# Encoder layer on one core: B's weights requested two ahead, and steps of the tail, the memory norm and cross attention moved

## The chip, the core and the metric

The kernel runs on one NeuronCore of a Trainium2 chip. The core has five engines that work side by side, each through its own queue, in order: TensorE (PE) multiplies matrices, and its weight loads (PEld) run ahead of the products; VectorE (DVE) and ScalarE (ACT) do elementwise work; GpSimd (POOL) here mostly issues DMAs; SyncE (SP) issues DMAs alone. An instruction that waits holds everything behind it on its engine. The metric is the device time of one execution in microseconds (us), less is better.

## The reference

One layer of an encoder on 256 frames (SEQ) of width 2048 (D), everything in float32:

```
h = LN(alpha*h + 0.5*SwiGLU_1(h))
h = LN(alpha*h + W_out[ sig(g_A)*(A(h) W_oA) + sig(g_B)*(B(h) W_oB) ])
h = LN(alpha*h + CrossAttn(h, LN(mem)))
h = LN(alpha*h + 0.5*SwiGLU_2(h))
```

A is chunked attention with a relative bias (16 heads of 64). B is latent attention (16 heads; queries and keys have 128 "nope" and 64 rotary columns, values 128). Queries, latents and gates of A and B come from one combined projection. Cross attention has 4 heads of 512 over 256 memory tokens, which get a layer norm of their own. The feed-forward layers are 5504 wide. Almost all the time goes into products of 256 rows with weight matrices that are each read once.

## The kernel before

**Weights.** Each weight matrix is cut into tiles of 128 x 2048 float32 (1 MB). `run` walks a list of items in the order in which they are to use weights. For weight number i, `fetch(i)` asks for the tile by a DMA on SP (L191) into one of three raw buffers (`wraw`). `load(i)` splits it: ACT casts it to a rounded high part in two pieces of 128 x 1024 (`hi`, L261), then DVE subtracts to get the low part (`lo`, L264). There are two pairs of buffers for hi and lo. PE multiplies hi with both halves of the activations and lo with the high half, which makes 24 products of 512 columns for a full weight ("a unit" below). Some weights go by named blocks instead of the two pairs; their tags name the blocks (X0 and X1, for example).

**Shared sums.** Some groups of weights use a Strassen-like product (`mm_sums`, L362), for which DVE first adds quarters of the weight (`weight_sums`, L245 and L247). The sums stand in a third raw buffer, or in a named block where the third entry of the tags names one; then they are cast to X2 (ACT) and X3 (DVE), like a weight.

**Totals and turns.** A product's two halves lie in PSUM. ACT copies one (L282) and DVE adds the other (L283); only then is the PSUM bank free. Four banks (`ps_mm`) and four more (`ps_at`) are used in rotation. Activations that must be turned are cut into 16-bit planes by ACT (`planes`, L839), sent by DMA transposes on SP (`send`, L843) and joined by ACT (`join`, L847).

**B's heads.** Items for the weights of queries' and keys' nope part (w_nope) and values (w_v) alternate with scores (L1026), softmax, turns and products with the values (L1080). While `early` is set, `load(i)` also asks for weight i + 1. Without it a weight is asked for when its load comes up.

**Cross attention.** In this order: keys 0 to 7, two query groups, value group 0, keys 8 to 15, value group 1, output projection. Side steps (sends, joins, `ready` which splits a head's queries, `scores`, `out`, and `gb`, which applies the residual's gain and bias to h) are put between the main steps by tables such as `{4: [join(0), scores(1)]}`: the number says ahead of which main step. The functions of the memory's norm are placed by a table too; `spread` multiplies ones with the diagonals of mean and scale (L1364), `quarter` applies them.

**What sets the order.** The program gives an order and priorities; a scheduler of the language then lays down the final order of each engine by its own costs. `issue_after` puts one instruction behind another one on the same engine.

Of the kernel before, what the change touches and what calls it, by code (L numbers as in the profile page):

```python
# [21 lines left out]
KT = D // P  # L22
# [15 lines left out]
AT_XQ = (4, 6), (2, 4, 6)  # L38
AT_XV = (2, 4, 6), (4, 6)
SUM_HOME = ("X2", "X3"),  # L40
# [59 lines left out]
class Kernel:  # L100
    def __init__(self, ctx, tc, t, out):
        self.tc, self.nc, self.t, self.out = tc, tc.nc, t, out

        def pool(name, bufs=1, **kw):
            return ctx.enter_context(tc.tile_pool(name=name, bufs=bufs, **kw))

        self.const = pool("const")
        self.wraw = pool("wraw", 3)
        self.whi = pool("whi", UNITS)
        self.wlo = pool("wlo", UNITS)  # L110
        self.blocks = pool("blocks")
        self.res = pool("res")
        self.work = pool("work", 4)
        self.small = pool("small", 4)
        self.ps_mm = pool("ps_mm", 4, space=PSUM)
        self.ps_at = pool("ps_at", 4, space=PSUM)
        self.items = []
        self.uid = 0
        self.chain = self.sent = None
        self.cut = self.early = False  # L120


# [54 lines left out]
    def run(self):  # L177
        queue = [w if isinstance(w, (tuple, Sums)) else (w, None) for _, ws, _, _ in self.items for w in ws]
        ready, nxt, live = [], 0, 0

        def slots(w):
            return 0 if isinstance(w, tuple) and w[1] else 1

        raws, sums = {}, {}

        def fetch(i):
            if i not in raws:
                ap = queue[i].ap if isinstance(queue[i], Sums) else queue[i][0]
                raws[i] = self.raw_tile()
                with self.tc.issue_after(self.sent.ins) if self.sent is not None else nullcontext():  # L190
                    self.last_load = self.nc.sync.dma_start(raws[i][:, :ap.shape[1]], ap)  # L191
            return raws[i]

        def form_sums(i):
            if i < len(queue) and isinstance(queue[i], Sums) and i not in sums:
                raw, home = fetch(i), queue[i].stage
                sums[i] = self.weight_sums(raw, queue[i].m, self.block(home, (P, 2048)) if home else self.raw_tile())

        def load(i):
            w = queue[i]  # L200
            raw = fetch(i)
            form_sums(i)
            if isinstance(w, Sums):
                n = 4 * w.m
                got = self.halves(raw[:, w.m:n], *self.unit()), self.halves(
                    sums[i][:, :n], *(self.block(g, (P, 2048), F32R) for g in w.tags))
            else:
                ap, tags = w
                hi, lo = (self.block(g, (P, 2048), F32R) for g in tags[:2]) if tags else self.unit()
                with self.tc.issue_after(self.ln_act.ins) if tags and "turned" in tags else nullcontext():  # L210
                    got = self.halves(raw[:, :ap.shape[1]], hi, lo)
            form_sums(i + 1)
            if self.early and i + 1 < len(queue):
                fetch(i + 1)
            return got

        def early(w):
            return not isinstance(w, Sums) and w[1] is not None and "early" in w[1]

        def ahead(need, held):  # L220
            if nxt < need:
                return True
            n = sum(not early(w) for w in queue[need:nxt])
            return (nxt < need + 5 and (early(queue[nxt]) or n < 2)
                    and held + live + slots(queue[nxt]) <= UNITS)

        done, highs = 0, []
        for fn, ws, held, prio in self.items:
            need = done + len(ws)
            while nxt < len(queue) and ahead(need, held):  # L230
                live += slots(queue[nxt])
                ready.append(load(nxt))
                highs.append(self.last_hi)
                nxt += 1
            got = [ready.pop(0) for _ in ws]
            live -= sum(slots(queue[done + i]) for i in range(len(ws)))
            done = need
            self.next_hi = highs[min(done, nxt - 1)] if highs else None
            self.now_hi = highs[done - 1] if done else None
            with self.prio(prio):  # L240
                fn(*got)
# [563 lines left out]

    def skewed(self, part, steps, tags=None):

        tags = tags or (None, None, ("X0", "X1"), ("X2", "X3"))
        held = [sum(g is None for g in tags[:j]) for j in range(5)]
        for j in range(4):  # L810
            part(0, j, tags=tags[j], held=held[j], keep=True)
        main = self.collect(lambda: [part(1, j, held=held[4] - held[j], again=True) for j in range(4)])
        self.weave(main, dict(zip((0, 3, 4), steps)))
# [516 lines left out]
    def mem_norm(self):  # L1330
# [46 lines left out]
                self.split(v, e["mT"].blk(0, 4 * q, 4), e["mT"].blk(1, 4 * q, 4))  # L1377
            return fn

        return {0: [load], 3: [stat], 6: [spread], 7: [quarter(0)], 9: [quarter(1)], 11: [quarter(2)], 13: [quarter(3)]}  # L1380

    def cross(self, xT, st, steps, steps_out):
        nc, t, e = self.nc, self.t, self.mem
# [15 lines left out]
        def query(g):  # L1399
# [16 lines left out]

            def join(tt):
                return lambda: [self.join(qs["add"][tt, a], turned[g][:, a, tt, :], 512) for a in range(2)]
            self.pair_group(g, t["w_xq"][g], 512, KT, xT, AT_XQ[g], fq, ps, qs)
            self.add(done, prio=SOON)  # L1420
            return {2: [send(0)], 3: [send(1)], 4: [join(0)], 5: [join(1)]}

        def ready(h):
            def fn():
# [7 lines left out]
        def val(g):  # L1432
            ps, qs = {}, {}

            def done():
                for a in range(2):
                    h = 2 * g + a
                    v[h] = self.block(VALUES[h], (P, 2, 2, X_DIM), F32R)
                    for tt in range(2):
                        p = qs["add"][tt, a]  # L1440
                        nc.vector.tensor_tensor(p, p, ps[tt, a], ALU.add)
                        self.split(p, v[h][:, 0, tt, :], v[h][:, 1, tt, :])
            self.pair_group(0, t["w_xv"][g], 512, KT, m, AT_XV[g], fv, ps, qs, None,
                            (("T0", "T1"),) if g else SUM_HOME)
            self.add(done, prio=SOON)

        def scores(h):
# [63 lines left out]
        def keys(a, b):  # L1511
            for j in range(a, b):
# [3 lines left out]
        side = group(query, {1: [form_q(4)], 3: [form_q(6)], 6: [form_q(2)]}, 0)  # L1516
        side = group(query, both(side, {4: [form_v(2)]}), 1)
        group(val, both(side, {2: [form_v(4)], 4: [form_v(6)]}), 0)
        group(keys, {0: [ready(0)], 1: [scores(0), gb(0)], 2: [ready(1), send(0)], 4: [join(0), scores(1)],
                     5: [out(0), ready(2)], 6: [send(1), gb(1)], 7: [gb(2)], 8: [join(1), ready(3), gb(3)]}, 8, KT)  # L1520
        group(val, {1: [out(1), scores(2)], 2: [scores(3)], 3: [send(2)], 4: [send(3)], 5: [join(2)], 6: [join(3)]}, 1)

        def all_items():
            self.out_pair(1, t["w_xo"][0], 0, KT, x, SUMS_XO, fx, True, st, (("T0", "T1"), "T3"))
# [170 lines left out]
```

## Time and profile before

| | us |
|---|---|
| three runs | 2445.43, 2444.67, 2443.38 (median 2444.67) |
| profiled execution | 2444.7 |
| its span | 2442.9 |
| PE busy | 2423.4 (99%) |
| DVE busy | 2121.5 (87%) |
| ACT busy | 1535.3 (63%) |

The span runs from the first instruction to the last. A busy PE means that some product is in flight. PE's idle time of some 20 us is the sum of the stretches in which it waited, the start and the end among them. The table of waits gives for each engine, line and releaser the idle time just before the instruction. DMA engines were busy some 60% of the time with the loads of SP's queue. The granted clock of the run was 0.997 of full.

### The profile page before, as it was taken

The page shows a single profiled execution, that of the slowest core. Times are in us where ns is not written, and L with a number is a line of the kernel's source. Part 1 is how long each engine was busy: PE and PEld are TensorE (multiplying, and loading weights), DVE is VectorE, ACT ScalarE, POOL GpSimd, SP SyncE. Part 2 cuts the span into 40 slices and gives each one's busy share as a digit, 9 for nine tenths or more (in the row PEclk, how much of TensorE's full clock was granted, in tenths as well). Part 3 has the DMA queues.
Part 4 walks back from the last instruction along what each step waited for, and adds up shares of the span by engine and source line. Part 5 has one row for each costly group of instructions (what it writes and reads, how often), then busy time and mean ns, then how long its engine had stood idle before and what let it go on. Part 6 is the DMA issues. An engine that isn't in the chain of part 4 may idle for free.

```text
span 2442.9 us, 29725 instructions
## 1 busy us (share of the span) xinstructions
PE 2423.4 (99%) x11314; PEld 2027.0 (83%) x11314; DVE 2121.5 (87%) x2428; ACT 1535.3 (63%) x2002; POOL 38.7 (2%) x83
## 2 busy tenths in 40 slices
PE   9999999999999999999999999999999999999997
PEld 8888888888888888888888888888888888888886
DVE  8999989899778997788789789889879999888996
ACT  6676755666555557878565567665666675557662
POOL 0000000000000001000000000000000000000000
PEclk9999999999999999999999999999999999999999
DMA  7766656667646657766676556655556766666664
GB/s 267 252 216 216 206 203 210 223 188 233 229 168 207 218 196 241 237 184 170 207 256 224 190 190 198 218 193 185 188 198 216 227 223 207 222 212 204 205 220 165
DMA packets 165854, 513.57 MB, mean 210 GB/s; under 512 B 101168, under 2 KB 101936, under 8 KB 110544
## 3 DMA queue, kind: packets, MB, share of 16 engines
q1 hardware_dynamic: 160256, 493.20, 60.6%
q0 software_dynamic: 4592, 17.30, 2.2%
q8 instruction: 88, 1.44, 0.2%
q10 hardware_dynamic: 864, 1.18, 0.1%
q14 instruction: 54, 0.44, 0.1%
HBM read 485.30 MB, written 2.10 MB: 200 GB/s over the span
## 4 chain that ended last, share of the span: by engine, by line
PE 92%; DVE 3%; ACT 2%; DMA 1%; issue 1%; SPq 0%; DVEq 0%; ACTq 0%; POOL 0%; POOLq 0%
PE at L308 26%; PE mm L308 25%; PE at L362 11%; PE mm L362 11%; PE mm L295 9%; PE mm L274 4%; PE mm L276 2%; ACT hi L261 1%; DVE lo L264 1%; PE at L1026 1%; DMA raw<-w_xk 0%; PE at L416 0%; ACT w L825 0%; PE at L1453 0%; PE at L1080 0%
## 5 line engine op out<-in xcount | busy, mean ns | idle before, releaser
L261 ACT CAST hi<-raw 128x1024 fp32r<-128x1024 f32 (+1 forms) x852 | 804.7, 982 | 466.6 <-PE at L308 157.3
L264 DVE TENSOR_TENSOR lo<-raw,hi 128x2048 fp32r<-128x2048 f32 (+1 forms) x427 | 903.2, 2116 | 148.9 <-ACT hi L261 144.2
L308 PE MATMUL mm<-hi,T 128*128 128x512 f32 (+1 forms) x1328 | 310.8, 384 | 0.0
L308 PEld LDWEIGHTS mm<-hi,T 128*128 128x128 f32 x1328 | 247.6, 188 | 46.5 <-ACT hi L252 0.3
L308 PE MATMUL at<-hi,T 128*128 128x512 f32 x1152 | 275.5, 389 | 0.0
L261 ACT CAST X<-H 128x1024 fp32r<-128x1024 f32 (+1 forms) x166 | 170.7, 1034 | 163.5 <-DVE H L245 129.9
L308 PEld LDWEIGHTS at<-hi,T 128*128 128x128 f32 x1152 | 216.2, 188 | 45.1
L264 DVE TENSOR_TENSOR X<-H,X 128x2048 fp32r<-128x2048 f32 (+1 forms) x83 | 186.9, 2252 | 68.5 <-ACT X L261 68.5
L308 PE MATMUL mm<-lo,T 128*128 128x512 f32 (+1 forms) x664 | 160.4, 382 | 0.0
L308 PEld LDWEIGHTS mm<-lo,T 128*128 128x128 f32 x664 | 123.7, 188 | 22.8
L308 PE MATMUL at<-lo,T 128*128 128x512 f32 x576 | 142.4, 389 | 0.0
L308 PE MATMUL at<-hi,H 128*128 128x512 f32 x560 | 133.7, 389 | 0.0
L308 PEld LDWEIGHTS at<-lo,T 128*128 128x128 f32 x576 | 108.1, 188 | 22.4
L308 PEld LDWEIGHTS at<-hi,H 128*128 128x128 f32 x560 | 105.0, 188 | 21.6
L308 PE MATMUL mm<-hi,H 128*128 128x512 f32 x480 | 114.8, 390 | 1.0 <-DVE w L283 1.0
L247 DVE TENSOR_TENSOR H<-H,raw 128x512 f32<-128x512 f32 (+1 forms) x166 | 112.6, 679 | 2.2
L308 PEld LDWEIGHTS mm<-hi,H 128*128 128x128 f32 x480 | 89.7, 188 | 19.8 <-DVE w L283 1.4
L245 DVE TENSOR_TENSOR H<-raw 128x1024 f32<-128x1024 f32 (+1 forms) x83 | 99.6, 1200 | 1.3 <-DMA raw<-w_gate 0.8
L261 ACT CAST X<-raw 128x1024 fp32r<-128x1024 f32 (+1 forms) x60 | 61.7, 1036 | 56.0 <-DVE raw L247 40.7
L362 PE MATMUL mm<-X,X 128*128 128x512 f32 x342 | 91.1, 392 | 0.0
L362 PE MATMUL at<-X,X 128*128 128x512 f32 (+1 forms) x315 | 82.4, 386 | 0.4 <-ACT X L261 0.4
L264 DVE TENSOR_TENSOR X<-raw,X 128x2048 fp32r<-128x2048 f32 (+1 forms) x30 | 67.5, 2254 | 15.0 <-ACT X L261 13.9
(353 smaller groups left out, 4115.0 us busy)
## 6 DMA issues: line engine op xcount, KB each, us to landing
raw<-ffn_w_in SPq DMA_DIRECT2D x150, 1024.0 KB, 4.9
raw<-ffn_w_out SPq DMA_DIRECT2D x66, 1024.0 KB, 4.9
raw<-w_gate SPq DMA_DIRECT2D x32, 1024.0 KB, 4.8
raw<-ffn_w_out_r SPq DMA_DIRECT2D x16, 1024.0 KB, 5.0
raw<-w_qk SPq DMA_DIRECT2D x16, 1024.0 KB, 5.8
raw<-w_o_b SPq DMA_DIRECT2D x16, 1024.0 KB, 4.9
raw<-w_out SPq DMA_DIRECT2D x16, 1024.0 KB, 4.8
raw<-w_xk SPq DMA_DIRECT2D x16, 1024.0 KB, 5.0
```

The source lines that it names most:

```text
L245: self.nc.vector.tensor_tensor(two[0], two[1], raw[:, :m].unsqueeze(1).to_broadcast([P, 2, m]), ALU.add)
L247: self.nc.vector.tensor_tensor(t[:, a * m:a * m + m], t[:, b * m:b * m + m], raw[:, a * m:a * m + m], ALU.add)
L261: self.last_hi = self.nc.scalar.copy(hi[:, c:d], src[:, c:d])
L264: self.last_lo = self.nc.vector.tensor_tensor(lo[:, :n], src, hi[:, :n].bitcast(F32), ALU.subtract)
L274: self.nc.tensor.matmul(ps, hi[j], x.both(kt), start=(j == 0), stop=False)
L276: self.last_mm = self.nc.tensor.matmul(ps[:, :S], lo[j], x.at(0, kt), start=False, stop=(j == n - 1))
L295: self.last_mm = self.nc.tensor.matmul(ps, x.at(xi, kt)[:, tt * P:(tt + 1) * P], w[wi][:, j * 512 + c:j * 512 + c + m], start=(start and j ...
L308: self.last_mm = self.nc.tensor.matmul(ps[tt, g][:, :n], x.at(xi, kt)[:, tt * P:(tt + 1) * P], w[wi][:, c:c + n], start=first and j + wi + ...
L362: self.last_mm = self.nc.tensor.matmul(bank[:, :m], a[xi], v[wi][:, c * m:(c + 1) * m], start=own and first and wi + xi == 0, stop=own and ...
L1026: nc.tensor.matmul(ps[:, c0:c0 + nk], q[:, tt * P:(tt + 1) * P], k[:, :nk], start=(j == 0), stop=(j == len(parts) - 1))
```

## The change

It has six parts, and no matmul is added or taken away.

1. In B's heads `load(i)` asks for weights i + 1 and i + 2 instead of i + 1 alone.
2. A third tag "next" puts a block's casts behind the last cast of the weight before it (`last_hi`). It is given to the two last weights of the shifted tail of ffn2.
3. In the memory's norm `spread` and the four quarters come one step later.
4. In cross, the sums of query group 0 stand in block H4 and those of value group 0 in block T2, where both stood in a raw buffer.
5. Sends and joins of a query group go to steps 1, 3, 4, 6 (were 2, 3, 4, 5).
6. The side steps of keys 8 to 15 and value group 1 are dealt out anew: scores(0) and gb(0) one step later, gb(1) two earlier, gb(2) one earlier, ready(3) and gb(3) among the values.

The diff, with nothing left out but context:

```diff
@@ run, load(i)
             else:
                 ap, tags = w
                 hi, lo = (self.block(g, (P, 2048), F32R) for g in tags[:2]) if tags else self.unit()
-                with self.tc.issue_after(self.ln_act.ins) if tags and "turned" in tags else nullcontext():
+                first = {"turned": self.ln_act, "next": self.last_hi}.get(tags[2]) if tags and len(tags) > 2 else None
+                with self.tc.issue_after(first.ins) if first else nullcontext():
                     got = self.halves(raw[:, :ap.shape[1]], hi, lo)
             form_sums(i + 1)
-            if self.early and i + 1 < len(queue):
-                fetch(i + 1)
+            for k in range(i + 1, min(i + 3, len(queue)) if self.early else 0):
+                fetch(k)
             return got
@@ skewed
-        tags = tags or (None, None, ("X0", "X1"), ("X2", "X3"))
+        tags = tags or (None, None, ("X0", "X1", "next"), ("X2", "X3", "next"))
@@ the memory's norm
-        return {0: [load], 3: [stat], 6: [spread], 7: [quarter(0)], 9: [quarter(1)], 11: [quarter(2)], 13: [quarter(3)]}
+        return {0: [load], 3: [stat], 7: [spread], 8: [quarter(0)], 10: [quarter(1)], 12: [quarter(2)], 14: [quarter(3)]}
@@ cross, query
-            self.pair_group(g, t["w_xq"][g], 512, KT, xT, AT_XQ[g], fq, ps, qs)
+            self.pair_group(g, t["w_xq"][g], 512, KT, xT, AT_XQ[g], fq, ps, qs, None,
+                            SUM_HOME if g else SUM_HOME + ("H4",))
             self.add(done, prio=SOON)
-            return {2: [send(0)], 3: [send(1)], 4: [join(0)], 5: [join(1)]}
+            return {1: [send(0)], 3: [send(1)], 4: [join(0)], 6: [join(1)]}
@@ cross, val
-                            (("T0", "T1"),) if g else SUM_HOME)
+                            (("T0", "T1"),) if g else SUM_HOME + ("T2",))
@@ cross, the order
-        group(keys, {0: [ready(0)], 1: [scores(0), gb(0)], 2: [ready(1), send(0)], 4: [join(0), scores(1)],
-                     5: [out(0), ready(2)], 6: [send(1), gb(1)], 7: [gb(2)], 8: [join(1), ready(3), gb(3)]}, 8, KT)
-        group(val, {1: [out(1), scores(2)], 2: [scores(3)], 3: [send(2)], 4: [send(3)], 5: [join(2)], 6: [join(3)]}, 1)
+        group(keys, {0: [ready(0)], 2: [scores(0), gb(0)], 3: [send(0), ready(1)], 4: [gb(1)], 5: [join(0), scores(1)],
+                     6: [out(0), ready(2), send(1), gb(2)], 8: [join(1)]}, 8, KT)
+        group(val, {1: [out(1), ready(3), scores(2)], 3: [send(2), scores(3), gb(3)], 5: [join(2), send(3)],
+                    7: [join(3)]}, 1)
```

In the new code lines from 208 to 1418 stand one further down (L843 becomes L844), those of cross attention two and the last ones three. The rows below name tiles by the program's names with their numbers.

SP's queue in the last heads of B, before. The load raw_8883 is the w_nope weight that is issued at 1114.78 us.

```order
L843 DMA_TRANSPOSE w_1331_8617<-H_1303_8465 128x6x128
L843 DMA_TRANSPOSE w_1344_8675<-H_1303_8465 128x6x128
L191 DMA raw_8769<-w_nope 128x2048
L843 DMA_TRANSPOSE w_1353_8725<-H_1303_8465 128x6x128
L843 DMA_TRANSPOSE w_1367_8789<-H_1303_8465 128x6x128
L191 DMA raw_8883<-w_nope 128x2048
L843 DMA_TRANSPOSE w_1376_8839<-H_1303_8465 128x6x128
L191 DMA raw_8945<-w_v 128x2048
L843 DMA_TRANSPOSE w_1389_8896<-T_1392_8909 128x6x128
```

The same stretch after; the numbers of the tiles are higher by two or fewer, since tiles are named when they are asked for.

```order
L844 DMA_TRANSPOSE w_1332_8619<-H_1304_8467 128x6x128
L844 DMA_TRANSPOSE w_1345_8677<-H_1304_8467 128x6x128
L191 DMA raw_8771<-w_nope 128x2048
L844 DMA_TRANSPOSE w_1354_8727<-H_1304_8467 128x6x128
L844 DMA_TRANSPOSE w_1368_8791<-H_1304_8467 128x6x128
L191 DMA raw_8885<-w_v 128x2048
L844 DMA_TRANSPOSE w_1377_8841<-H_1304_8467 128x6x128
L191 DMA raw_8947<-w_nope 128x2048
```

Each load has moved into the place of the one before it: the weight that was raw_8883 is now raw_8771, between the same transposes where the weight before it stood.

ACT's last casts of ffn2, before; X_2917 and X_2920 are the blocks of the last two weights.

```order
L261 CAST hi_18918<-raw_18916 128x1024 x2
L261 CAST hi_18947<-raw_18945 128x1024 x2
L261 CAST X_2917_18987<-raw_18985 128x1024
L261 CAST hi_18980<-raw_18978 128x1024 x2
L261 CAST X_2917_18987<-raw_18985 128x1024
L261 CAST X_2920_19006<-raw_19004 128x1024
```

The same casts after:

```order
L262 CAST hi_18918<-raw_18916 128x1024 x2
L262 CAST hi_18947<-raw_18945 128x1024 x2
L262 CAST hi_18980<-raw_18978 128x1024 x2
L262 CAST X_2917_18987<-raw_18985 128x1024 x2
L262 CAST X_2920_19006<-raw_19004 128x1024
```

The casts hi_18980 have moved ahead of the first cast of X_2917.

DVE at the change from keys to value group 1, before. w_1985 and w_1992 are the totals of keys 14 and 15, lo_12851 and lo_12904 the first two weights of the value group, X_1998 the queries of head 3.

```order
L264 TENSOR_TENSOR lo_12851<-raw_12848,hi_12850 128x2048
L283 TENSOR_TENSOR w_1985_12843<-w_1985_12843,mm_12810 128x256
L253 TENSOR_TENSOR w_1997_12910<-w_1964_12666,w_1996_12909 128x512
L253 TENSOR_TENSOR X_1965_12668<-w_1985_12843,X_1965_12668 128x256
L253 TENSOR_TENSOR X_1998_12913<-H_1877_12059,X_1998_12913 128x4x128 x2
L458 TENSOR_TENSOR h_101<-h_101,w_1999_12918 128x512
L283 TENSOR_TENSOR w_1992_12896<-w_1992_12896,mm_12863 128x256
L264 TENSOR_TENSOR lo_12904<-raw_12901,hi_12903 128x2048
```

The same place after; key 14's total is now w_1987, the first lo lo_12859, the queries of head 3 X_2010.

```order
L265 TENSOR_TENSOR lo_12859<-raw_12856,hi_12858 128x2048
L284 TENSOR_TENSOR w_1987_12851<-w_1987_12851,mm_12818 128x256
L254 TENSOR_TENSOR w_1997_12910<-w_1972_12720,w_1996_12909 128x512
L254 TENSOR_TENSOR X_1960_12633<-w_1987_12851,X_1960_12633 128x256
L265 TENSOR_TENSOR lo_12904<-raw_12901,hi_12903 128x2048
L284 TENSOR_TENSOR w_1992_12896<-w_1992_12896,mm_12863 128x256
L254 TENSOR_TENSOR X_2010_12985<-H_1877_12059,X_2010_12985 128x4x128
```

The splits of head 3's queries and the first step of gb(3) have left the place ahead of key 15's total, and the second lo has moved ahead of it.

2 lines of the change are left out of this document (1 added, 1 removed).

## Prediction

> **What bounds the kernel.** The page comes first: how much of the span each engine works, and which engine the chain that ended last runs through.
>
> ```profile
> PE 2423.4 (99%) x11314; PEld 2027.0 (83%) x11314; DVE 2121.5 (87%) x2428; ACT 1535.3 (63%) x2002; POOL 38.7 (2%) x83
> ...
> PE 92%; DVE 3%; ACT 2%; DMA 1%; issue 1%; SPq 0%; DVEq 0%; ACTq 0%; POOL 0%; POOLq 0%
> ```
>
> TensorE is the bound from end to end: 2423.4 of 2442.9 us. The change adds and removes no matmul, so it can win only idle time of PE or time at a lowered clock, and can lose only by making new idle time. I read the table of PE's waits next; each row is us in total, times, longest.
>
> ```profile
> PE at L1026 <- DVE w L283: 2.2, 2, 1.9
> PE mm L295 <- DVE lo L264: 1.1, 1, 1.1
> ...
> PE mm L308 <- DVE w L283: 1.0, 1, 1.0
> PE at L362 <- DVE X L264: 0.8, 1, 0.8
> PE at L1453 <- DVE T L253: 0.4, 1, 0.4
> ...
> PE at L1364 <- DVE w L1357: 0.3, 1, 0.3
> ```
>
> These six rows hold 5.8 us, and I looked up each in time: 1128.78 (B's heads), 2414.86 (ffn2's tail), 1608.68, 1545.80 and 1560.69 (cross), 1323.03 (the memory's norm). All six lie where the diff touches. The first has an aftermath, which the table by stretches shows (PEclk is the figure ahead of the last two).
>
> ```profile
> 1128.00:1134.00 6.00, 5.22 (x20) 4.42 (x21) 6.00 (x16) 4.48 (x10) 0.54 (x1) 0.72 0.51 171
> ...
> 1606.00:1612.90 6.90, 5.89 (x28) 4.56 (x27) 6.83 (x10) 4.20 (x7) 0.00 (x0) 1.00 0.53 167
> ```
>
> Right after the 1.9 us wait the granted clock was 0.72 over 6 us, so (1 - 0.72) x 6.00 = 1.7 us of matmul time went there. The second stretch holds the wait of 1.0 us at 1608.68 and shows 1.00: a wait of that size cost itself alone.
>
> **The change, part by part.** *B's weights asked for two ahead.* Rows of the timeline by engine, and the landing of the one late load from the chain:
>
> ```profile
> 1103.32 0.57 SPq L191 DMA_DIRECT2D raw<-w_nope  x1
> 1106.74 7.99 SPq L843 DMA_TRANSPOSE w<-H  x2
> 1114.78 0.57 SPq L191 DMA_DIRECT2D raw<-w_nope  x1
> 1123.83 1.21 SPq L843 DMA_TRANSPOSE w<-T  x1
> ...
> 1114.78 7.22 DMA raw<-w_nope
> ...
> 1118.69 0.59 ACT L1146 COPY X<-mm 128x512 f32<-128x512 f32 x1
> 1122.02 1.05 ACT L261 CAST hi<-raw 128x1024 fp32r<-128x1024 f32 x1 [2.74 <-DMA raw<-w_nope]
> ...
> 1116.63 2.29 DVE L264 TENSOR_TENSOR lo<-raw,hi 128x2048 fp32r<-128x2048 f32 x1
> 1124.79 2.29 DVE L264 TENSOR_TENSOR lo<-raw,hi 128x2048 fp32r<-128x2048 f32 x1 [2.61 <-ACT hi L261]
> ...
> 1128.78 0.49 PE L1026 MATMUL at<-w,w 128*128 128x128 f32 x2 [1.93 <-DVE w L283]
> ```
>
> The load stood on SP behind two transposes that waited for their planes, landed at 1122.00, and held ACT 2.74 us, then DVE 2.61 us; the totals L283 that PE wanted stood on DVE behind that subtract of 2.29 us. In the new order this load has the place of the one at 1103.32, 11.5 us earlier; even at 7.22 us it lands by 1110.6. What ends last is then ACT's own queue: the casts stand there around the copy of 1118.69, so hi is there by about 1121.3 and lo by 1123.7, 3.4 us sooner than 1127.1, against 1.93 to be gained. What was hidden stays hidden: DVE did the subtract beside PE. The wait goes, and with it the lowered clock: 1.9 + 1.7 = 3.6 us. What is late next on SP is the transposes, now behind loads; see the rivals. The smaller wait in the same row (0.3) I leave.
>
> [...]
>
> *Tags "next" in ffn2's tail.* ACT's rows, then the chain:
>
> ```profile
> 2409.53 1.05 ACT L261 CAST X<-raw 128x1024 fp32r<-128x1024 f32 x1 [4.37 <-DMA raw<-ffn_w_out_r]
> 2410.49 1.99 ACT L261 CAST hi<-raw 128x1024 fp32r<-128x1024 f32 x2
> ...
> 2412.51 2.30 DVE lo L264
> 2414.86 3.24 PE mm L295 x13
> ```
>
> ACT stood 4.37 us before the X0 cast, which waited for a raw tile, while the next weight's hi casts were queued behind. Now these go first, as soon as PE has left the weight before last and so freed their buffer. PE wanted the weight at 2414.86 - 1.1 = 2413.8 and had begun the one before it one weight (24 matmuls of 0.23, 5.4 us) earlier, so that is about 2408.4; casts 2.0, lo 2.3: ready at 2412.7 instead of 2414.81, 1.1 before PE wants it. X0's first cast then starts at about 2410.4, 0.9 us later, and that weight is used after this one, so PE's work on it covers the delay; without the cover it would cost those 0.9. Term: 1.1 us.
>
> *The memory's norm one step on.* The chain there:
>
> ```profile
> 1322.70 0.29 DVE w L1357
> 1323.03 0.49 PE at L1364 x2
> ```
>
> PE reached the ones x diag products 0.3 us before the diagonals were there. One weight later (5.4 us) they are long ready. The quarters follow one step later too; only the first key of cross wants them, after a step count that is still some weights on, so PE's units of the mixer's tail cover that. 0.3 us.
>
> *Cross: staging in H4 and T2, joins and sends moved.*
>
> ```profile
> 1540.70 1.35 ACT L847 COPY H<-w 128x1024 uint16<-128x1024 uint16 x1
> 1542.37 1.05 ACT L261 CAST X<-raw 128x1024 fp32r<-128x1024 f32 x1 [0.32 <-DVE raw L247]
> ...
> 1543.45 2.29 DVE L264 TENSOR_TENSOR X<-raw,X 128x2048 fp32r<-128x2048 f32 x1 [1.12 <-ACT X L261]
> ...
> 1545.80 0.96 PE L362 MATMUL at<-X,T 128*128 128x512 f32 x3 [0.75 <-DVE X L264]
> ...
> L362 PE MATMUL at<-X,T x9: 389/389/500, 1543.1 to 1546.4; 128*128 128x512 f32 x9
> ```
>
> The last sums of val(0) came 0.75 us late because two joins of 1.35 us stood among ACT's casts. The two joins of this stretch now stand behind both X casts and the next hi, and the block T2 leaves a third raw tile for loads; the subtract should end near 1543.4 instead of 1545.7: 0.75 us. The sends of both query groups now put two transposes ahead of two weight loads on SP. At worst those hold SP as in row 1106.74 (7.99 for two, with their wait for planes); the data are wanted about one weight (5.4 us) after they used to land, so the price lies between nothing and 2.6 us for each group. I take nothing: here the planes are done before the send, and PE's unit in between covers the rest.
>
> *Cross: scores(0) one key later.*
>
> ```profile
> 1559.43 1.22 DVE T L253 x2
> 1560.69 2.42 PE at L1453 x18
> ```
>
> The query splits L253 end at 1560.65; PE now starts scores(0) after key 9, near 1562.4. 0.4 us.
>
> *Cross: the first unit of val(1).* Its four PSUM banks are those of keys 12 to 15.
>
> ```profile
> 1578.09 3.04 PE L1453 MATMUL at<-X,T 128*128 128x256 f32 x24
> ...
> 1590.82 1.23 SPq L843 DMA_TRANSPOSE w<-w  x1
> ...
> raw<-w_xv SPq DMA_DIRECT2D x1, 1024.0 KB, 7.0
> ...
> raw<-w_xk SPq DMA_DIRECT2D x16, 1024.0 KB, 5.0
> ...
> 1608.20 0.42 DVE L283 TENSOR_TENSOR w<-w,mm 128x256 f32<-128x256 f32 x1
> 1608.54 2.29 DVE L264 TENSOR_TENSOR lo<-raw,hi 128x2048 fp32r<-128x2048 f32 x1
> ...
> 1608.68 2.57 PE L308 MATMUL mm<-hi,H 128*128 128x512 f32 x10 [1.01 <-DVE w L283]
> ```
>
> Before, key 15's total (1608.20) came ahead of the second lo (1608.54). In the new order it stands behind it, which costs 2.2 us there, while ready(3) (two splits like those of 1559.43, 1.2 us) and gb(3) have left DVE's queue ahead of it, and PE now does 13 matmuls (0.23 us each, 2.57 for 10 with the drain) before the fourth bank instead of six. Walking it: scores(1) ends at 1584.9 (it ended at 1581.1; one key of 5.5 comes ahead of it, less the 1.5 of the waits gone); planes and transposes at about 1591 to 1592; the w_xv load 1.3 us on, landing 5.0 to 7.0 later, so 1597.5 to 1600.2. From there two casts (2.0), lo (2.2), key 14's total and split (0.7), two casts (2.0), lo and total (2.5) make 9.4: the bank is free at 1606.9 to 1609.6. PE began this unit at 1608.68 - 1.01 - 6 x 0.23 = 1606.3, now 1.5 sooner, 1604.7; it wants the bank at 1604.7 + 13 x 0.23 = 1607.7. A wait of 0 to 2.1; I take 0.6, nearer the quick end since the loads of gains and biases for gb no longer run then. Term: 0.4 us gained, between 1.0 gained and 1.1 lost.
>
> **Sum.** 3.6 + 1.1 + 0.3 + 0.75 + 0.4 + 0.4 = 6.55. The matmul behind a wait takes 500 instead of 389 ns (row of X above), 0.11 for each of five waits that go: 0.55. Together 7.1. The profiled run took 2444.7 us, the median of the runs is 2444.67, so 2444.7 - 7.1 = 2437.6. No bound of the known terms reaches zero; together they lie between 5.6 (val(1) at its worst) and 7.7.
>
> **Rivals.**
> 1. *val(1)'s fourth bank takes the place of B's wait.* If the w_xv load takes 7 us the wait is 2.1, above the 1.9 that was followed by the lowered clock: 1.5 more than I took, and 1.7 of clock. 2437.6 + 3.2 = 2440.8. For it: the order on DVE. Against: it takes the slow landing and every earlier unit on time. Chance 0.16.
> 2. *The dip of the clock is not B's wait.* Then it comes at some other place: 2437.6 + 1.7 = 2439.3. For it: one case only is seen. Against it: it begins within a us of the longest wait of the kernel, and the shorter ones show none. Chance 0.08. [...]
> 3. *Two ahead is one ahead.* wraw has three tiles; the unit in work and two ahead take all, so the new request may wait for the lo of the unit before, which row 1116.63 is an instance of. Then the load goes out hardly sooner and B keeps its 3.6 and the 0.11: 2441.3. Against: the late load issued at 1114.78, as the transposes (1106.74 + 7.99) let go, so its tile had been free. Chance 0.08.
> 4. *Slower: the transposes wait behind the loads.* SP is a queue, and in B a load that waits for a raw tile now stands ahead of a pair of transposes at four places. If the tile comes free after the planes, the heads' joins and their products come late; at 1.9 + 1.7 for each, four make 14.4: 2437.6 + 14.4 = 2452.0. It ends slower by over 0.2% only if the four lose more than 12 us, 3 each. Against: the tile for the load ahead of the transpose of 1123.83 is free at 1118.9 (1116.63 + 2.29), 4.9 us sooner. Chance 0.07.
>
> **Chances and range.** The forecast has 0.61. What a measurement can tell from no change is 0.2%, 4.9 us: faster means below 2439.8. Forecast and rival 2 fall there (0.69); rivals 1 and 3 are within 0.2% (0.24); slower is rival 4 (0.07). The range starts at 2436.0 (all terms at their upper bound, 2437.0, and a us for the smaller waits in the same stages) and reaches over rivals 2, 1 and 3 to 2442.0; left out are rival 4 and the tails of the others.
>
> **What would show it.** Right: no wait at L1026 (new line 1027) above 0.5 us, and PEclk 1.00 from 1125 to 1131; no wait of mm L295 in the last 40 us; at L1453, L1364 and L362 (new 1455, 1365, 363) none over 0.2; one at the fourth bank of 0 to 2. Wrong: a row "PE ... <- DVE w L283" (new line 284) near 1605 of 2 us with a PEclk under 1.00 behind it, or waits for ACT H L847 in B's heads, or DMA raw<-w_xq, w_xv as a releaser in cross. I would be wrong altogether if PE's idle time in B moved instead of vanishing.

## The result, and the profile after

The changed kernel takes 2437.07 us (median of 13 runs, 2436.64 to 2442.3), the kernel before, run beside it, 2444.92 us (13 runs, 2441.83 to 2448.9). The ratio of the means is 0.9971 with a 95% interval of 0.9963 to 0.9980: faster by 0.29%, which is more than the 0.2% that can be told from no change, by a little. The profiled run took 2436.7 us with a span of 2434.9 us.

The page of the changed kernel, busy time and shares of the chain:

```profile
PE 2420.7 (99%) x11314; PEld 2024.9 (83%) x11314; DVE 2120.0 (87%) x2428; ACT 1534.3 (63%) x2002; POOL 38.9 (2%) x83
...
PE 91%; DVE 4%; ACT 3%; DMA 1%; issue 1%; SPq 0%; DVEq 0%; ACTq 0%
```

As many instructions on every engine as before; PE is busy 2.7 us less, of which 1.7 are those that it no longer spends at half clock in B. The table of PE's waits (us in total, times, longest) has lost five of the six rows that the prediction named. Of the sixth, the one of B's heads (now L1027), only the small wait is left, 0.2 us:

```profile
PE at L489 <- DVE w L466: 1.1, 1, 1.1
PE at L363 <- ACT X L262: 0.4, 2, 0.2
PE at L1081 <- ACT H L848: 0.2, 1, 0.2
PE at L1027 <- DVE w L284: 0.2, 1, 0.2
PE mm L309 <- ACT hi L253: 0.2, 1, 0.2
```

The stretch after B's old wait, by windows. Behind the window's length stand the busy times of PE, PEld, DVE, ACT and POOL. PE is busy throughout, and the granted clock (the figure ahead of the last two) is 1.00.

```profile
1125.00:1131.00 6.00, 6.00 (x38) 5.39 (x37) 5.87 (x16) 5.84 (x14) 0.54 (x1) 1.00 1.17 278
```

The queue of SP in the timeline of the same kernel shows how it came about. The load of w_nope that left at 1114.78 now leaves at 1102.96, ahead of the two transposes that hold SP for 8.00 us; what stands behind them at 1114.43 is the load of the weight after it. The load at 1118.59 then waits for a raw tile, and the transpose behind it leaves at 1121.50, without any wait of PE.

```profile
1102.96 0.57 SPq L191 DMA_DIRECT2D raw<-w_nope  x1
1106.38 8.00 SPq L844 DMA_TRANSPOSE w<-H  x2
1114.43 0.57 SPq L191 DMA_DIRECT2D raw<-w_v  x1
1115.10 1.37 SPq L844 DMA_TRANSPOSE w<-H  x1
1118.59 0.33 SPq L191 DMA_DIRECT2D raw<-w_nope  x1
1121.50 1.32 SPq L844 DMA_TRANSPOSE w<-T  x1
```

The chain in the tail of ffn2, one row for 12.24 us: no weight is waited for.

```profile
2399.93 12.24 PE mm L296 x54
```

To place the gain I took the matmul that started at the edge of each stretch, by its number in PE's order (every kernel has 11314), and compared its start in the two traces. The table gives how that difference changed over each stretch, in us against the profiled execution of before; minus is gained. The last five columns are kernels of the experiments below.

| stretch (us of before) | predicted | after | two ahead alone | tail and norm alone | cross: blocks alone | cross: steps alone | before, again |
|---|---|---|---|---|---|---|---|
| B, 1123 to 1134 | -3.7 | -3.79 | -3.79 | -1.56 | +0.03 | +0.09 | +0.07 |
| B, 1134 to 1185 | 0 | +0.68 | +0.65 | +0.57 | 0.00 | +0.03 | +0.28 |
| memory's norm, 1300 to 1354 | -0.4 | -0.57 | -0.59 | -0.59 | -0.34 | +0.30 | -0.25 |
| cross, val(0) and scores(0), 1541 to 1571 | -1.4 | -1.74 | +0.54 | -0.06 | -1.04 | -1.74 | -0.06 |
| cross, val(1), 1594 to 1620 | -0.4 | -0.92 | -0.42 | -0.48 | -1.19 | -0.95 | -0.37 |
| w_xo, 1620 to 1700 | 0 | +0.24 | 0.00 | 0.00 | 0.00 | +0.24 | 0.00 |
| tail of ffn2, 2412 to 2420 | -1.2 | -1.37 | -0.27 | -1.37 | -0.10 | -0.09 | -0.38 |
| all the rest | 0 | -0.52 | -0.44 | -0.17 | -0.37 | -0.26 | -0.17 |
| span | -7.1 | -7.99 | -4.32 | -3.66 | -3.01 | -2.38 | -0.88 |

The 0.11 us that the prediction gives to each restart of PE behind a wait (500 against 389 ns) is counted in its stretch. The last column is the same code as before, so a stretch that the edit doesn't touch moves by up to 0.4 us from one execution to the next, and the whole by about a us. Each column holds one execution; in medians the kernel with two ahead alone gains 2.96 us, less than its column shows.

A time in one trace can't be set beside a time in another as it stands, since PE is at another point of its work there. At 1594 us of before, the kernel after is 5.76 us ahead, the one with the blocks alone 1.61 and the one with the steps alone 1.56.

### The profile page after: what moved, and what is told of

It reads as the page before. It is cut to its first block, busy times and chain, and to the rows that moved or that the text cites. A ratio compares the mean times of both kernels' runs of the same rounds, so it can differ in the third digit from the quotient of the medians.

```text
span 2434.9 us, 29728 instructions
## 1 busy us (share of the span) xinstructions
PE 2420.7 (99%) x11314; PEld 2024.9 (83%) x11314; DVE 2120.0 (87%) x2428; ACT 1534.3 (63%) x2002; POOL 38.9 (2%) x83
## 4 chain that ended last, share of the span: by engine, by line
PE 91%; DVE 4%; ACT 3%; DMA 1%; issue 1%; SPq 0%; DVEq 0%; ACTq 0%
PE at L309 25%; PE mm L309 25%; PE at L363 11%; PE mm L363 11%; PE mm L296 10%; PE mm L275 5%; PE mm L277 2%; DVE lo L265 2%; ACT hi L262 1%; PE at L1027 1%; DMA raw<-w_xv 0%; PE at L417 0%; DMA raw<-w_xq 0%; PE at L1081 0%; ACT H L848 0%
## 5 line engine op out<-in xcount | busy, mean ns | idle before, releaser
L262 ACT CAST X<-raw 128x1024 fp32r<-128x1024 f32 (+1 forms) x50 | 51.1, 1034 | 45.5 <-DVE raw L248 34.7
L848 ACT COPY w<-w 128x1024 uint16<-128x1024 uint16 (+1 forms) x60 | 75.7, 1275 | 1.4 <-DMA w<-w 1.4
```

What stands on the lines that cost most here:

```text
L262: self.last_hi = self.nc.scalar.copy(hi[:, c:d], src[:, c:d])
L848: self.nc.scalar.copy(self.words(u, n).rearrange("p (c k) -> p k c", k=2), self.words(s, n).rearrange("p (k c) -> p k c", k=2))
```

## Experiments

**Two ahead, alone.** The kernel before with the first edit only:

```diff
-            if self.early and i + 1 < len(queue):
-                fetch(i + 1)
+            for k in range(i + 1, min(i + 3, len(queue)) if self.early else 0):
+                fetch(k)
```

> The kernel before with part 1 alone (B's weights asked for two ahead). My theory: the wait of 1.9 us at L1026 goes and the lowered clock behind it too, so the span is some 3.1 to 3.7 us shorter than before (2442.9), the stretch of B's heads has a PEclk of 1.00, and the other five waits (1.1 in the tail, 1.0 and 0.8 and 0.4 in cross, 0.3 at the norm) stand as before. Rival (the lowered clock does not hang on this wait): the wait goes, 1.9 us are won, and a stretch of 3.4 us at half clock shows up somewhere else. Rival (the tile, not the queue, made the load late): nothing changes.

Measured: 2441.82 us (10 runs), ratio 0.9988 (0.9978 to 0.9997), span 2438.6. Its waits of PE:

```profile
PE at L362 <- DVE X L264: 1.0, 1, 1.0
PE mm L295 <- DVE lo L264: 0.8, 1, 0.8
PE at L1453 <- DVE T L253: 0.7, 1, 0.7
PE mm L308 <- DVE w L283: 0.6, 1, 0.6
...
PE at L1026 <- DVE w L283: 0.2, 1, 0.2
```

B's wait of 1.9 us is gone, the waits of cross and of the tail stand there as before. So this edit is the whole of B's gain. The wait of the memory's norm (L1364) is gone too, though the norm was not moved.

**The tail and the norm, alone.** The kernel before with `("X0", "X1", "next"), ("X2", "X3", "next")`, the casts put behind the last hi, and the norm's spread and quarters one step on. The two lie far apart, and each is read from its own stretch.

> The kernel before with the tag next in ffn2's tail and the memory's norm one step on, nothing else. My theory: the wait of 1.1 us for lo in the tail goes (a gain of 1.1 to 1.4 us between the middle of ffn2 and its end) and the 0.3 us at L1364 goes (0.3 to 0.6 us there); B's wait with its lowered clock and the three of cross stay. Span about 1.5 to 2.0 us under 2442.9. Rival (the tail is held by the landing of its last loads): the wait of 1.1 us comes back one weight later as a wait for X0 or X2, and the tail gains nothing.

Measured: 2441.0 us (one run), span 2439.2, a gain of 3.7 us where I had expected 1.5 to 2.0. The wait at B is where it was, but the clock behind it is 1.00:

```profile
PE at L1027 <- DVE w L284: 2.2, 2, 2.0
```

```profile
1125.00:1131.00 6.00, 4.02 (x25) 3.48 (x24) 6.00 (x15) 4.05 (x10) 0.48 (x1) 1.00 0.64 202
```

(These are its waits and its windows.) So 1.56 us of this kernel's gain is a dip of the clock that did not come, with the wait in place: the dip does not follow this wait each time, as I took it to. The tail gained 1.37 us.

**The kernel before, a second time.**

> The kernel before, unchanged, a second time. It asks how much of the 8.0 us between the two spans belongs to the code. In the kernel with only the tail and the norm changed, B's wait of 2.0 us stood in its place but the granted clock stayed at 1.00 behind it. Theory 'the wait brings the dip each time': the wait of 1.9 to 2.0 us at the heads of B, PEclk 0.7 to 0.9 from 1126 to 1134, span 2442 to 2444. Rival 'a wait of that size brings the dip in some executions only': the same wait, and either a dip of 1.7 us or none at all, in which case the span is 2440.5 to 2442. In both the waits of cross are there again within 0.3 us of 0.75 (sums of val(0)), 0.4 (query splits) and 0.6 to 1.0 (fourth bank of val(1)).

Measured: 2443.78 us, span 2442.0. The wait of 2.0 us is followed by the dip again; the windows of this execution:

```profile
1124.86:1128.28 3.42, 1.45 (x10) 1.17 (x10) 3.42 (x8) 1.47 (x4) 0.00 (x0) 1.00 0.91 272
1128.28:1131.69 3.41, 3.41 (x11) 2.86 (x12) 2.93 (x9) 3.41 (x8) 0.54 (x1) 0.50 0.23 90
```

Five executions have this wait with 1.9 to 2.0 us (before twice, tail and norm, and the two cross kernels below). Four had the dip (0.72 from 1128 to 1134 in each), one had not (1.00). The late subtracts below show what lay ahead of some other dips, but not why this one stayed away.

**Cross: the blocks alone.** The kernel before, with H4 and T2 for the sums:

```diff
-            self.pair_group(g, t["w_xq"][g], 512, KT, xT, AT_XQ[g], fq, ps, qs)
+            self.pair_group(g, t["w_xq"][g], 512, KT, xT, AT_XQ[g], fq, ps, qs, None,
+                            SUM_HOME if g else SUM_HOME + ("H4",))
...
-                            (("T0", "T1"),) if g else SUM_HOME)
+                            (("T0", "T1"),) if g else SUM_HOME + ("T2",))
```

> The kernel before, with only the two blocks H4 and T2 for the splits of the sums in cross; joins, sends, query splits and the rest stay in their old steps. Theory 'the joins are the cause of the late subtract of val(0)': its wait stays at 0.6 to 1.0 us, the two others of cross (0.25 to 0.65 and 0.5 to 1.0) stay, the span is 2441 to 2443.5 and the ratio 0.9995 to 1.0005. Rival 'the raw tile is the cause': the wait of val(0) falls under 0.3 us, the weights of cross are asked for earlier, and 0.5 to 1 us goes.

Measured: 2441.67 us (10 runs), ratio 0.9993 (0.9983 to 1.0002), span 2439.9. The total alone can't be told from no change; the waits can be read. Neither the row of val(0)'s sums (L362 for DVE X) nor that of val(1)'s fourth bank (mm L308 for DVE w) is left; the one for the query splits stays:

```profile
PE mm L295 <- DVE lo L264: 0.9, 1, 0.9
PE at L362 <- ACT X L261: 0.4, 2, 0.2
PE at L1454 <- DVE T L253: 0.4, 1, 0.4
```

The loads of w_xv leave earlier. The first row is of before and the second of this kernel, both ahead of val(0); the third, also of this kernel, is ahead of val(1):

```profile
1528.15 9.93 SPq L191 DMA_DIRECT2D raw<-w_xv  x3
```

```profile
1522.84 7.18 SPq L191 DMA_DIRECT2D raw<-w_xv  x3
1587.31 10.24 SPq L191 DMA_DIRECT2D raw<-w_xv  x3
```

PE is 0.57 us ahead of before at 1541 and 1.61 at 1594, so against PE the loads of val(0) are 4.7 us earlier, and that of val(1), at 1592.10 in before, 3.2. The joins were in their old steps and the subtract of val(0) was in time all the same: with a raw tile set free, the order of the joins doesn't matter. The rival came true; my reason (the joins among the casts) was not needed.

**Cross: the steps alone.** The sends, joins, scores, splits, gains and side steps of the kernel after, with the sums in raw tiles as before:

```diff
-            return {2: [send(0)], 3: [send(1)], 4: [join(0)], 5: [join(1)]}
+            return {1: [send(0)], 3: [send(1)], 4: [join(0)], 6: [join(1)]}
```

(and the two lines of `group(keys, ...)` and `group(val, ...)` as in the change).

> The kernel before, with only the steps of cross moved (sends, joins, scores, query splits, gains and biases, side steps), the sums still staged in raw tiles. Theory 'the steps do it': the waits of 0.75 at val(0)'s sums and 0.4 at scores(0) go, that of val(1)'s fourth bank is 0 to 1.2, and 1 to 2 us go between 1540 and 1620; ratio 0.9992 to 0.9997. Rival 'the steps need the blocks': the loads of w_xv and w_xq wait for a raw tile, the fourth bank or a hi comes 1 to 3 us late, and the stretch gains less than 0.5 us or loses.

Measured: 2442.27 us (10 runs), ratio 0.9994 (0.9984 to 1.0004), span 2440.5. The waits of val(0) and scores(0) are gone, and the fourth bank is waited for by 0.07 us. The load of w_xv leaves at 1593.01, where the kernel after has 1588.33; but PE starts key 14 at 1593.43 here and at 1589.23 there (second fence), so against PE it is only 0.5 us later than in the kernel after:

```profile
1591.72 1.24 SPq L843 DMA_TRANSPOSE w<-w  x1
1593.01 3.92 SPq L191 DMA_DIRECT2D raw<-w_xv  x3
1593.43 3.82 PE L274 MATMUL mm<-H,hi 128*128 128x512 f32 x16
```

```profile
1589.23 3.82 PE L275 MATMUL mm<-H,hi 128*128 128x512 f32 x16
```

Against before, where the load left at 1592.10 and key 14 started at 1594.99, the steps make it 2.5 us later.

So blocks and steps each clear the waits of val(0) and of val(1)'s bank by themselves: -1.04 and -1.19 us by the blocks, -1.74 and -0.95 by the steps, -1.74 and -0.92 together. Only scores(0) needs the steps. The steps alone also bring the 0.24 us lost at w_xo.

**The last splits and gains back.** The kernel after, with `ready(3)` and `gb(3)` again in step 8 of the keys:

```diff
-                     6: [out(0), ready(2), send(1), gb(2)], 8: [join(1)]}, 8, KT)
-        group(val, {1: [out(1), ready(3), scores(2)], 3: [send(2), scores(3), gb(3)], 5: [join(2), send(3)],
+                     6: [out(0), ready(2), send(1), gb(2)], 8: [join(1), ready(3), gb(3)]}, 8, KT)
+        group(val, {1: [out(1), scores(2)], 3: [send(2), scores(3)], 5: [join(2), send(3)],
```

> The kernel after, with the last splits of the query and the last gains and biases put back to where they stood, among the keys ahead of val(1). They are 1.2 us of DVE's work ahead of the fourth bank's total. Theory 'that work sets the fourth bank's time': its wait comes back with 0.6 to 1.3 us (0.1 in the kernel after), all else as after, span 2435.4 to 2436.5. Rival 'the earlier load does': the load of w_xv lands at about 1594 as in the kernel after, the wait stays under 0.3, span 2434.7 to 2435.4.

Measured: 2437.26 us (one run), span 2435.5; the stretch of val(1) is 1.23 us shorter than before (0.92 in the kernel after) and its chain is PE alone:

```profile
1601.44 5.55 PE mm L309 x24
```

With the blocks, that work of DVE costs nothing where it stood, so this move brought nothing here. The span is 0.6 us above that of the kernel after; the shifts put more than that, 0.9, ahead of B, at the start of the program.

**Sends and joins back.** The kernel after with `{2: [send(0)], 3: [send(1)], 4: [join(0)], 5: [join(1)]}` for the query groups.

> The kernel after, with the sends and joins of cross's query groups back in steps 2, 3, 4 and 5. They were costed at nothing (between nothing and 2.6 us for each group). With the blocks alone the subtract of val(0) was already in time, the joins in their old place. Theory 'blocks and moved joins do the same thing twice': span 2434.2 to 2435.6, no wait over 0.3 us from 1535 to 1565. Rival 'the moved joins are needed once the rest is moved': a wait of 0.4 to 0.8 at the sums of val(0), span 2435.6 to 2436.3. Rival 'the moved sends cost something': 0.5 to 1 us faster than the kernel after.

Measured: 2437.27 us (one run), span 2435.5. Cross is as in the kernel after (-1.74 and -1.16 us in its two stretches), and what the span is longer by lies ahead of B, where PE waited 0.7 us for an instruction to issue. Moving the sends and joins costs nothing and brings nothing beside the blocks.

**Three ahead.** The kernel after with `min(i + 4, len(queue))`.

> The changed kernel with B's weights asked for three ahead instead of two; there are three raw tiles. My theory (rival 4 of the prediction, brought about): the third request waits on SP for the subtract of the unit in work and holds transposes behind it, so joins in B's heads come late; I expect PE waits for ACT H L848 or for totals of 1 to 4 us in all in B, the time 1 to 6 us over that of the changed kernel, with a lowered clock if one of the waits reaches 1.9 us. Rival (transposes are ready later than the tiles in any case): the time of the changed kernel, within 1 us, and the same short table of waits.

Measured: 2437.67 us (6 runs, 2436.56 to 2438.31), ratio to before 0.9969 (0.9957 to 0.9981), span 2436.1. Now a load that waits for a tile stands ahead of the pairs of transposes in B's heads, which is the fourth rival in its full form:

```profile
1109.48 0.33 SPq L191 DMA_DIRECT2D raw<-w_v  x1
1109.90 6.49 SPq L844 DMA_TRANSPOSE w<-H  x2
```

Its price in the waits:

```profile
PE at L1081 <- ACT H L848: 0.6, 2, 0.3
PE at L417 <- issue: 0.5, 1, 0.5
...
PE at L1081 <- ACT T L848: 0.3, 1, 0.3
```

Three waits of the products for the joined planes, 0.85 us together, where the rival had four of 1.9 with a dip behind each. The kernel after has one of 0.2. So my expectation of 1 to 4 us of waits and 1 to 6 of time was too dear: the medians differ by 0.6 us.

**None ahead.** The kernel before without any early request in B.

> The kernel before without asking ahead in B at all, each weight when its load comes up. My theory: each load of B now stands one place later on SP, behind the transposes of the next step too, so PE waits in several places of B's heads, some 3 to 8 us each, the span 10 to 40 us longer; and behind each wait of 1.9 us or more the granted clock is at half for about 3.4 us, behind those of 1.1 us or less it is not. [...] Rival (the load was late for want of a tile): hardly any change.

Measured: 2448.77 us (one run), span 2447.0, so the request one ahead that the kernel before had was worth some 4 us, not the 10 to 40 that I had expected. Its largest row of waits:

```profile
PE mm L272 <- ACT hi L259: 3.5, 2, 1.8
```

The two waits in this row were of 1.62 us (no dip behind it: 1.00 from 1121 to 1125) and 1.83 us (a dip: 0.50 from 1152 to 1154).

**Two raw tiles.** The kernel after with `pool("wraw", 2)`.

> The kernel after, with two raw tiles instead of three. Theory 'two ahead lives on the third tile': a load in B waits for the lo of the unit before, the wait of the heads at 1128 comes back with at least 1.5 us, waits for hi or raw appear there of 1 to 4 us each, and over the whole kernel 10 to 80 us are lost. Rival 'the third tile was idle': the span is within 3 us of 2434.9, and two ahead was one ahead.

Measured: 2579.84 us (one run), span 2578.1: 143 us lost, over the whole kernel and more than the 80 of my expectation. The first row below lies in heads of A (products of 64 columns, at 1050.05 and 1134.50); the second is that of the heads of B, two waits for joined planes:

```profile
PE at L1081 <- ACT w L848: 4.4, 2, 2.6
...
PE at L1081 <- ACT T L848: 2.0, 2, 1.5
```

It says that the third tile is in use, but since every stage lost it, it prices that and not the edit; the rows of SP above answer the third rival better.

**Late subtracts.** The kernel after, with the subtract of every twelfth weight done one, two or three times more, with the same values:

```diff
+            self.nth = getattr(self, "nth", 0) + 1
+            more = (2, 1, 3, 2)[self.nth // 12 % 4] if n == 2048 and self.nth % 12 == 0 else 0
+            for _ in range(1 + more):
                 self.last_lo = self.nc.vector.tensor_tensor(lo[:, :n], src, hi[:, :n].bitcast(F32), ALU.subtract)
```

> The kernel after, with the subtract that makes lo done again (the same values) one, two or three times at every twelfth weight, 2.2 us each: 59 more subtracts, 130 us of DVE, at 29 places. It makes waits of PE of many lengths, to see which of them the lowered clock follows. So far, of seven waits of 1.6 to 2.0 us at the heads of B, five were followed by 3.4 us at half clock, and none of some thirty of 1.2 us or less. Theory 'length and chance': no dip behind waits up to 1.3 us, a dip behind some of those from 1.5 to 2.2 us, behind all from 3 us on, and each dip costs 1.5 to 1.9 us. Rival 'the dip belongs to the heads of B': no dip outside them, however long the wait. [...] Span 2470 to 2560, since DVE has 13% of its time free.

Measured: 2524.74 us (one run), span 2522.8, with 64 more subtracts and 136 us more of DVE. Two of its waits have the same length, 2.65 us, at 1018.43 and 415.19, and differ in what follows. Its windows, cut from the start of a dip in steps of 3.413 us (the length of the dip in the clock record of before):

```profile
1016.33:1019.74 3.41, 2.10 (x10) 1.40 (x8) 3.41 (x5) 3.41 (x10) 0.71 (x3) 1.00 0.33 115
1019.74:1023.16 3.42, 2.08 (x17) 2.08 (x18) 3.42 (x8) 3.42 (x8) 0.00 (x0) 1.00 0.34 74
1023.16:1026.57 3.41, 3.41 (x26) 2.58 (x26) 3.41 (x7) 2.90 (x6) 0.00 (x0) 1.00 0.88 286
415.58:419.00 3.42, 1.15 (x5) 0.98 (x6) 3.42 (x4) 1.04 (x2) 0.00 (x0) 1.00 0.13 29
419.00:422.41 3.41, 3.41 (x10) 2.62 (x9) 3.41 (x3) 1.90 (x3) 0.00 (x0) 0.50 0.94 363
```

The wait at 1018.43 lies across a cut: 1.31 us idle in one window, 1.34 in the next, and no dip. That at 415.19 lies almost wholly in one window, 2.27 us of it, and the next window runs at half clock from end to end. The kernel with two tiles has the opposite case, two waits of 1.13 us of which 1.97 us lie in one window, with a dip behind them:

```profile
294.85 0.97 PE L363 MATMUL at<-X,X 128*128 128x512 f32 x3 [1.13 <-DVE X L265]
...
297.17 1.04 PE L309 MATMUL mm<-hi,H 128*128 128x512 f32 x2 [1.13 <-ACT hi L262]
```

```profile
294.00:297.41 3.41, 1.44 (x5) 0.92 (x6) 1.39 (x2) 1.34 (x2) 0.00 (x0) 1.00 0.88 315
297.41:300.82 3.41, 3.41 (x9) 2.62 (x9) 2.69 (x2) 1.92 (x3) 0.00 (x0) 0.50 0.37 154
```

Neither theory above says this. Dips came outside the heads of B (at 419.00 here, at 297.41 in the kernel with two tiles), behind 2.27 and 1.97 us of idle time in a window, and the length of a wait alone did not decide. The section on the hardware sets the windows of these executions side by side.

## Why the prediction came true, point by point

The time was forecast as 2437.6 us with a range of 2436.0 to 2442.0, and is 2437.07. The sum was 7.1 us. Against the profiled execution of before the span fell by 7.99, against the second execution of the same code by 7.1 (2442.0 - 2434.9), so the total can't be known better than to about a us, and its agreement is partly luck: the stretches of its terms gained 1.3 us more than forecast, mostly in the four besides B's, two losses of 0.9 in all were not in it, and 0.5 came from elsewhere.

- **B's wait and its clock, 3.6 us.** Right in place, in what the earlier request does, and in size for the pair of executions compared: 3.79 us between 1123 and 1134, and the kernel with this edit alone has the same 3.79. But 1.7 of it is a dip that comes behind this wait in four executions of five, not always. The second rival asked whether the dip is B's wait at all. In the kernel after, with two ahead alone, with three ahead, and with the splits or the sends put back, the wait is gone. In the first three of these every stretch of 20 us up to 1660 was granted 1.00, and with the splits put back 1125 to 1134 was, so the dip goes with the wait; but the wait does not bring it each time, and what spared it once stays open.
- **What is late next.** I named the transposes behind loads, and took nothing for them. No wait of that kind came at the heads (the transpose behind the load that waited for a tile left at 1121.50 and was in time), but 0.68 us was given back between 1134 and 1185. Only a part can be named: PE, now earlier, waits 0.15 us at 1162 for planes whose join stands on ACT right behind another copy of planes (1160.31) and ends at 1162.10, which with the dearer restart (0.70 us for the two products, 0.59 for the two at 1160.04) is 0.26. The two rows are of ACT and of PE in the kernel after:

```profile
1161.04 1.06 ACT L848 COPY T<-w 128x768 uint16<-128x768 uint16 x1
```

```profile
1162.15 0.70 PE L1081 MATMUL at<-T,X 128*128 128x256 f32 x2
```

  The kernel with the tail and the norm alone gives back 0.57 at the same place with no request moved, so it isn't the new order of SP alone, and the unchanged kernel's second execution gives back 0.28 there. The rest came in small steps among the products of the last heads; what makes them stays open.
- **The tail, 1.1 us and a restart.** Right: 1.37, in the kernel after and in the one with that edit, against 0.1 to 0.4 in kernels without it.
- **The memory's norm, 0.3 us.** The wait went, but the term is not shown to be the move's. In the five executions with neither edit the wait was 0.3 (before) and 0.6 us (steps), and absent from the table of waits in the other three (before again, none ahead, blocks); with two ahead or with the move it is absent each time. In the kernel with two ahead alone the last diagonal starts 0.22 us after PE's first of these products (1318.69 and 1318.47), in before 0.78 after (1322.70 and 1321.92). So the first edit already removes the wait, and so do other executions of the old code; what the move itself is worth stays open.
- **val(0), 0.75 us, and scores(0), 0.4.** Size right (1.74 with two restarts, against 1.4). The cause I named, two joins among ACT's casts, is one of two that each suffice; the blocks clear the wait with the joins left as they were. The query splits need the steps, as said.
- **val(1)'s fourth bank.** The walk held; only the wait that I picked from its range was too long. PE of the kernel after is 5.76 us ahead of before here, of which the walk had counted 1.5, so 4.26 us have to be added to the times of the trace to set them beside the walk's. Rows of SP's timeline and of the chain:

```profile
1587.04 1.24 SPq L844 DMA_TRANSPOSE w<-w  x1
1588.33 3.91 SPq L191 DMA_DIRECT2D raw<-w_xv  x3
```

```profile
1588.33 5.47 DMA raw<-w_xv
...
1600.93 2.29 DVE lo L265
...
1603.60 2.79 PE mm L309 x11
```

  With 4.26 added, the transpose left at 1591.3 (walk: 1591 to 1592), the load landed at 1598.1 (1597.5 to 1600.2), the bank was free at 1607.8 (1606.9 to 1609.6) and PE wanted it at 1607.8 (1607.7). The walk's end of scores(1), 1584.9, is a slip for 1585.1 (1581.1 + 5.5 - 1.5). The load took 5.47 us, near the quick end, so the wait was 0.1 us instead of 0.6, and the gain 0.9 instead of 0.4. The kernel with the steps alone shows the same: its load landed in 4.96 us, and the wait was 0.07. The first rival's condition, a landing of 7 us, did not come up, so no run shows what it would have cost.
- **Not in the sum.** 0.2 to 0.3 us lost at w_xo, in every kernel with the moved steps, and 0.5 gained outside the edit. Of the latter 0.6 lies near 680, where a wait of 0.3 for the issue of an instruction was there in the kernel before and not after; the second execution of before lacks it too, so it is no work of the change.
- **The rivals.** The third (two ahead is one ahead) fell: the load left 11.8 us earlier, 11.5 against PE. The fourth fell by size: with a waiting load ahead of the pairs of transposes PE loses 0.85 us.

## What to carry to other kernels

A kernel whose bound engine is 99% busy is improved wait by wait, and each wait of half a us or more is worth looking up in time, since one of them cost nearly twice its length here through the clock (3.7 us for a wait of 2, in four executions of five). When several edits remove the same wait, only runs of each alone tell which did it: here blocks and steps in cross did the same work twice, and at the norm the wait was gone before the edit that was meant for it. When two traces are compared, a time counts against PE's own place in its work: two loads that left 4.7 us apart were 0.5 us apart in that sense. Where a gain of parts is summed, run the unchanged kernel's profile a second time first: it showed here which tenths of a us are no one's doing.

## What the runs showed of the hardware

In the stretches listed here the half clock lasted 3.41 us, or twice that, and the length of a wait alone did not decide whether it came. The dip of before is 3.413 us long in its clock record: 0.50 from 1129.67 to 1133.08, with 1.00 on both sides. In the kernel with late subtracts 0.50 was granted from 419.00, 1958.41, 2101.77 and 2105.18 on, the last two without a break. The second and the third of these lie 1539.41 and 1682.77 us behind the first, which is 451 and 493 times 3.413 to within 0.2 us. The table has PE's idle time in stretches of 3.41 us at full clock (their length less the busy time), and the clock of the 3.41 us behind each:

| kernel | stretch from (us) | PE idle (us) | clock behind it |
|---|---|---|---|
| late subtracts | 1954.99 | 2.45 | 0.50 |
| late subtracts | 415.58 | 2.27 | 0.50 |
| before, again | 1124.86 | 1.97 | 0.50 |
| two raw tiles | 294.00 | 1.97 | 0.50 |
| tail and norm alone | 1126.35 | 1.94 | 1.00 |
| before | 1126.26 | 1.93 | 0.50 |
| late subtracts | 2098.35 | 1.93 | 0.50 |
| late subtracts | 555.53 | 1.85 | 1.00 |
| two raw tiles | 1007.38 | 1.83 | 1.00 |
| late subtracts | 1019.74 | 1.34 | 1.00 |
| late subtracts | 1016.33 | 1.31 | 1.00 |

In these rows half clock followed 1.93 us and more, but for one, and none followed 1.85 us and less. A limit between the two is not shown: with no request ahead a dip came behind a wait of 1.83 us. One stretch that was itself at half clock was followed by another one, with 0.87 us idle (2101.77, late subtracts). One execution does not fit: with the tail and norm alone, the stretch worked out from its clock records has 1.94 us of idle time from 1126.35 on, and no dip; why stays open. The dip at B's heads in before cost (1 - 0.72) x 6.00 = 1.68 us. So B's wait of 2 us cost 2 us once and 3.7 four times, and the idle time does not explain the one (1.92 to 1.98 us in the 6 us around the wait in all five); the two waits of 2.65 us above do differ by how they lie to the cuts (1.31 and 1.34 us in two windows and no dip, 2.27 in one and a dip).
